# A decoder layer's next low-rank transposition behind the decays' sums, and its gated weights split right behind their scaling

## The chip, the cores and the metric

One core of one Trainium2 chip runs the whole program in one launch. The metric is device microseconds of one execution, all inputs in HBM at its start and all outputs in HBM at its end. The kernel before took 2267.43 us, the median of 3 runs (2267.4 to 2267.67).

## The reference

One layer of a hybrid decoder on 2048 prompt tokens and 8 × 8 sample tokens, model width 1024. One input projection feeds two groups of heads: A is sliding-window attention with rotary positions and a learned sink for each head, B is gated linear attention (GLA: 4 heads, keys of 64, values of 128). Their outputs are joined, projected and added to the input; a squared-ReLU MLP of 4096 follows.

```python
proj = jnp.einsum('btd,de->bte', rms_norm(x, g_mix_pre), w_in)
q, k, v, gq, gk, gv, gr, glr = jnp.split(proj, points, axis=-1)      # glr: 16 columns
attn = swa_banded(q, k, v, sinks)                                    # group A, window 128
log_a = log_sigmoid(einsum('btr,rk->btk', glr, w_gk2) + b_gk) / 16   # GLA's decays, low rank
o, s_new = gla_chunked(gq, gk, gv, log_a, s_init)
gla_out = rms_norm(o, g_gla) * silu(gr)
x = x + rms_norm(concat(attn, gla_out) @ w_out, g_mix_post)
u = relu(rms_norm(x, g_ffn_pre) @ w_up)
x = x + rms_norm((u * u) @ w_down, g_ffn_post)
```

## The kernel before

All is fp32. A product is made of high and low parts: a factor is copied to a rounded type (hi, ACT), the rest is subtracted (lo, DVE or POOL), and three matmuls hi·hi, hi·lo, lo·hi are summed in PSUM. The prompt is 16 tiles of 128 tokens (numbers 0 to 15); the 64 sample tokens are tile 16 (NB).

**The stages.** First the attention stage, to about 342 us: for each tile the input projection of group A (proj), rotary, scores (sc), softmax (s), its transposition (pT), the weighted values (av). Then the GLA stage, to about 790 us. Then output projection, and the MLP's up and down products, the longest part. PE's, ACT's and DVE's order in the attention stage is the order of recording: `te`, `ac` and `dv` chain each instruction to the one before. Instructions issued on `nc.*` directly are placed by the scheduler, by what they depend on and the priority that the place in the program gives. `tc.issue_after(x)` holds a block's priority back behind x.

**The weights of group B in the attention stage.** Their columns are four chunks (c = 0 to 3, limits G_AT; chunk 3, of 400 columns, ends with the 16 low-rank ones). Chunks 3 and 0 (G_EARLY) are prepared during tiles 3 to 10, two pieces of 128 rows in each: `load_gw` asks for a raw piece (two raw buffers, SP's queue), `split_gw` (L264) multiplies it by the norm's gain on POOL (L269) and leaves the copy to hi (ACT) and the subtract to lo (POOL, L273) in the list `gained`; `split_some` (L757), called once in each of a tile's four units, first does what is in `gained`, then takes new pieces, (2, 1, 0, 0) by unit. So the copy and the subtract of a piece follow one call behind its multiply. On POOL there are also the casts of kh and kl (L436 to L447), which bring keys to the other half of the partitions, and the rotary products (L387, L393).

**GLA, one tile.** `decays` makes log-decays for a tile: the 16 low-rank columns of gp are transposed (pg), DVE casts them to glrT (L944), one matmul with w_gk2 gives z, ACT and DVE make the log-sigmoid zt, lh and ll (L953 to L956); `decayed` transposes zt (tT) and copies it to `before` (L1068). `gla(i)` makes keys and queries (gqk), sums decays with a matrix of ones (es) and takes their exp (kd, L1087), starts the output gate (sg, L962 to L971), and then walks seven levels b = 1, 2, … 64: `level_sums` extends the running sums `before` and `after` by adds on DVE (L1012, L1013) and takes exps on ACT (dec), `leveled` multiplies keys and queries by them (XK L994, XQ L998). At L1098 ACT takes the exp of all of `before`, from which DVE makes qd (L1100). The level products are matmuls in four groups (gm_0, gm_2, gm_4, gm_6, two levels each), and each result is put into AT by masked copies on DVE (L1019). Then ds, the state, and o. `following` is the next tile's `decayed`: it is advanced once behind each gm group, so the next tile's pg stands behind gm_0, z behind gm_2, tT behind gm_4.

**What lies between.** Each `yield` hands over to `fill`, which records G_FILL, G_GM matmuls of later tiles' projections to group B (gproj, chunk order 3, 0, 1, 2, tiles 16, 2, 3, … 15), and to `side`, the sample's own GLA (`gla_sample`: its decays are se, its other sums ses). `projecting` evicts a sample chunk in two ACT copies and one DVE add (L619 to L626). The fill ends in tile 13: the first chunk that it projects for tile 14 is not finished when tile 13's sums are recorded.

**Banks.** PSUM has tags a, b, c with two banks each, d and e with one. gproj takes a, the sample b, gm c; gqk, es, pg, z and ds share d; o and ogT share e; tT takes b.

**The output projection** takes its third tile's input by `load_mix`, whose split (hi by ACT, lo by DVE) is recorded while tile 15's levels run.

Of the kernel before, what the change touches and what calls it, by code (L numbers as in the profile page):

```python
# [15 lines left out]
AF = mybir.ActivationFunctionType  # L16
# [5 lines left out]
P = 128  # L22
# [7 lines left out]
HD = 64  # L30
# [95 lines left out]
def f32(ap):  # L126
    return ap.bitcast(F32)
# [23 lines left out]
def hybrid_step_kernel(ctx: ExitStack, tc: tile.TileContext, I, O):  # L151
# [97 lines left out]

    gw, gained = {}, deque()  # L250

# [12 lines left out]
    def split_gw(c, k, raw):  # L264
        hi, lo = (t[:, k, : g_width(c)] for t in gw[c][1:])
        if c in G_LATE:
            split_gained(hi, lo, raw, k)
            return
        nc.gpsimd.tensor_tensor(raw, raw, gcol[:, k : k + 1].to_broadcast([P, g_width(c)]), op=ALU.mult)  # L269

        def rest():
            ac.activation(hi, raw, AF.Copy)
            nc.gpsimd.tensor_tensor(lo, raw, f32(hi), op=ALU.subtract)  # L273

        gained.append(rest)

# [324 lines left out]
    def projecting(i, xT, chunks, act=nc.scalar):  # L601

        n = rows(i)
        for c in chunks:
            p_ = bank([P, 512], "a", f"gproj_{i}_{c}")
            _, wh, wl = gw[c]
# [150 lines left out]
    def split_some(n):  # L757

        while gained:
            gained.popleft()()  # L760
        for _ in range(min(n, len(weights))):
            c, k, raw, stage = weights.popleft()
            split_gw(c, k, raw)
            if stage and late:
                weights.append((*load_gw(*late.popleft(), *stage), stage))
# [171 lines left out]

    def decays(i, gp, n, kind="d"):

        assert {(i, c) for c in range(4)} <= projected or i < NB  # L940
        gt = glrT[i % 2] if i < NB else s_kx[:32, 0, :]
        pg = bank([P, P], kind, f"pg_{i}")
        te.transpose(pg[:16, :n], gp[:n, 1536:1552], ident[:n, :n])
        nc.vector.tensor_copy(gt[:16, :n], pg[:16, :n])  # L944
# [8 lines left out]
        nc.vector.scalar_tensor_tensor(t[:n], z[:n], 0.0, t[:n], op0=ALU.min, op1=ALU.subtract)  # L953
# [61 lines left out]
    def put_level(at, gm, mk, b, n):  # L1015

        dst = halves(at, b)[1]
        m = mk.rearrange("p (m b) -> p m b", b=b).unsqueeze(1).to_broadcast([n, 4, n // (2 * b), b])
        nc.vector.copy_predicated(dst, m, gm.rearrange("p h (m b) -> p h m b", b=b))  # L1019

# [37 lines left out]

    def decayed(i, gp):

        assert (i, 3) in projected
        parts = yield from decays(i, gp, P)
        yield
# [8 lines left out]
    def gla(i, gp, og=iter(())):  # L1072
# [14 lines left out]
        ex = nc.scalar.activation(kd, e_, AF.Exp, scale=1.0 / 16)  # L1087
        nc.gpsimd.tensor_tensor(kd, kd, gp[:, 256:512], op=ALU.mult)
        with tc.issue_after(ex.ins):
            sg = gate(i, gp, P)  # L1090
# [5 lines left out]
        yield G_FILL[1] if i < NB - 1 else G_LAST, 2  # L1096
        following = decayed(i + 1, gps[i + 1]) if i < NB - 1 else iter(())
        nc.scalar.activation(dec[:, :, NL, :], before, AF.Exp, scale=1.0 / 16)  # L1098
# [3 lines left out]
        for l0 in range(0, NL, 2):  # L1102
# [3 lines left out]
            for l in range(l0, min(l0 + 2, NL)):  # L1106
                for g in range(2):
# [5 lines left out]
                    for u, uu in enumerate(half_of):  # L1113
# [3 lines left out]
                        )  # L1117
            next(following, None)
            if l0 == NL - 1:
# [6 lines left out]
            for l in range(l0, min(l0 + 2, NL)):  # L1126
# [5 lines left out]
                for u, uu in enumerate(half_of):  # L1132
                    put_level(at[uu, :, uu], gm[uu, l - l0, :, u * 32 : u * 32 + 32], msk[uu, l, u * 32 : u * 32 + 32], LEVELS[l], HD)
        So, Sn = S[i % 2], S[(i + 1) % 2]
        for g in range(2):
            for r in range(2):
# [3 lines left out]
                    op0=ALU.mult, op1=ALU.add,  # L1140
                )
        yield G_FILL[2], 2
        o_ = bank([P, 4, P], "e", f"o_{i}")
# [17 lines left out]
    def gla_sample(gp):  # L1161
# [9 lines left out]
        qk = qk_T(i, gp, NS, "b")  # L1171
        yield
        for g in range(2):
            e_ = bank([P, (SL + 1) * NS], "b", f"se_{g}")
            te.matmul(e_, lh[:NS, g * P : (g + 1) * P], slev, start=True, stop=False)
            te.matmul(e_, ll[:NS, g * P : (g + 1) * P], slev, start=False, stop=True)
            nc.scalar.activation(s_dec[:, g].rearrange("p l t -> p (l t)"), e_, AF.Exp, scale=1.0 / 16)
        yield
# [60 lines left out]
    def load_mix(i, lo=None, hi=None):  # L1239
        n = rows(i)  # L1240
        if lo is not None:
            nc.sync.dma_start(f32(lo), mix_d[i])
            yield
            split_copy(hi, lo, f32(lo))
            mixes[i] = [[t[:, k, :] for k in range(KT)] for t in (hi, lo)]
# [119 lines left out]

    wo, pre, ogs_of, mixes, raws, late_mix = {}, {}, {}, {}, [], []
    early = []
# [3 lines left out]
    for i in range(NB):  # L1371
        parts = [gla(i, gps[i], ogs_of.pop(i - 1, iter(())))]
        if i == 0:
            parts = [(n or (12, True) for n in decayed(i, gps[i])), *parts]
        for n, free in chain.from_iterable(parts):
# [744 lines left out]
```

## Time and profile before

| | us |
|---|---|
| median of 3 runs | 2267.43 |
| profiled execution | 2268.25 |
| its span | 2266.5 |
| outside the span | 1.75 |
| PE busy | 2203.9 |
| DVE busy | 1621.2 |
| ACT busy | 1202.2 |
| POOL busy | 272.8 |

A row of the timeline has the start, the length of the instruction (or of so many together, x2), the engine, the line, the operation, what it writes and reads, and in brackets the idle time ahead of it and what ended it. L140 is the wrapper of the recorded engines, so there one reads by the tile's name. A row of the waits has total, count and longest. A row of the windows has for each engine its busy time, then the clock that was granted to PE (1.00 is full), the DMA share and GB/s. SPq is SyncE's queue, from which the transfers start.

### The profile page before, as it was taken

The page shows a single profiled execution, that of the slowest core. Times are in us where ns is not written, and L with a number is a line of the kernel's source. Part 1 is how long each engine was busy: PE and PEld are TensorE (multiplying, and loading weights), DVE is VectorE, ACT ScalarE, POOL GpSimd, SP SyncE. Part 2 cuts the span into 40 slices and gives each one's busy share as a digit, 9 for nine tenths or more (in the row PEclk, how much of TensorE's full clock was granted, in tenths as well). Part 3 has the DMA queues.
Part 4 walks back from the last instruction along what each step waited for, and adds up shares of the span by engine and source line. Part 5 has one row for each costly group of instructions (what it writes and reads, how often), then busy time and mean ns, then how long its engine had stood idle before and what let it go on. Part 6 is the DMA issues. An engine that isn't in the chain of part 4 may idle for free.

```text
span 2266.5 us, 34072 instructions
## 1 busy us (share of the span) xinstructions
PE 2203.9 (97%) x11800; PEld 1879.8 (83%) x11800; DVE 1621.2 (72%) x3367; ACT 1202.2 (53%) x2498; POOL 272.8 (12%) x424
## 2 busy tenths in 40 slices
PE   8989999999999999999999999999999999999997
PEld 7888888889998788888888888888888888888886
DVE  5888877888887776687776788878544645755557
ACT  5777764445545444455555565555444444554445
POOL 3466421112112110000000000000000000000000
PEclk9999999999999999999999999999999999999999
DMA  7333332121112355766454666676655755866665
GB/s 235 119 128 133 109 97 64 66 73 52 49 65 71 119 200 177 246 215 234 172 207 173 246 244 227 220 251 228 226 185 179 227 175 185 280 222 219 223 195 196
DMA packets 229938, 392.65 MB, mean 173 GB/s; under 512 B 23057, under 2 KB 137638, under 8 KB 225782
## 3 DMA queue, kind: packets, MB, share of 16 engines
q1 hardware_dynamic: 229766, 390.48, 51.5%
q8 instruction: 93, 1.52, 0.3%
q14 instruction: 79, 0.65, 0.1%
HBM read 255.61 MB, written 135.86 MB: 173 GB/s over the span
## 4 chain that ended last, share of the span: by engine, by line
PE 71%; DVE 16%; ACT 6%; DMA 3%; issue 3%; POOL 1%; SPq 0%; DVEq 0%; ACTq 0%; POOLq 0%
PE dn L140 24%; PE uc L140 7%; PE ua L140 7%; PE gproj L140 7%; PE out L1276 5%; PE ud L140 4%; PE ue L140 3%; PE ub L140 3%; DVE s L140 2%; PE proj L140 2%; DVE AT L1019 1%; PE sam L140 1%; PE dsam L140 1%; PE out L140 1%; DVE pl L140 1%
## 5 line engine op out<-in xcount | busy, mean ns | idle before, releaser
L140 PE MATMUL dn<-ot,os 128*128 128x512 f32 x2688 | 623.8, 390 | 3.6 <-DVE ot L140 2.0
L140 PEld LDWEIGHTS dn<-ot,os 128*128 128x128 f32 x2688 | 503.9, 188 | 113.0 <-DVE ot L140 5.3
L140 DVE TENSOR_TENSOR os<-os 128x512 fp32r<-128x512 f32 x224 | 154.8, 691 | 227.9 <-ACT os L140 227.5
L140 ACT ACTIVATE os<-os 128x512 fp32r<-128x512 f32 x224 | 141.4, 631 | 284.1 <-DMA os<-s_d 233.2
L140 PE MATMUL gproj<-wg,gx 128*128 128x384 f32 (+1 forms) x1408 | 280.7, 349 | 2.1 <-ACT s_dec L621 1.6
L140 PEld LDWEIGHTS gproj<-wg,gx 128*128 128x128 f32 x1408 | 247.8, 191 | 12.9 <-issue 10.7
L140 ACT ACTIVATE st<-st 128x512 f32<-128x512 f32 x225 | 142.3, 633 | 142.0 <-DVE st L140 137.9
L140 PE MATMUL ua<-H,w 128*128 128x512 f32 x744 | 179.8, 390 | 1.0 <-DVE w L140 0.9
L140 PE MATMUL uc<-H,s 128*128 128x512 f32 x744 | 178.8, 389 | 0.0
L140 PEld LDWEIGHTS ua<-H,w 128*128 128x128 f32 x744 | 138.5, 188 | 30.2 <-DVE w L140 1.8
L140 PEld LDWEIGHTS uc<-H,s 128*128 128x128 f32 x744 | 139.5, 188 | 28.9
L216 POOL TENSOR_TENSOR frs<-rs_v,half 128x1 f32<-128x1 f32 (+1 forms) x13 | 8.3, 636 | 1228.9 <-DVE rs_v L140 1228.9
L140 DVE TENSOR_TENSOR st<-st 128x512 f32<-128x512 f32 x160 | 110.4, 692 | 49.2 <-ACT st L140 45.9
L1276 PE MATMUL out<-wo,mt 128*128 128x512 f32 x608 | 141.8, 392 | 0.5 <-DVE mt L227 0.5
L1276 PEld LDWEIGHTS out<-wo,mt 128*128 128x128 f32 x608 | 113.1, 188 | 24.0 <-DVE mt L227 1.0
L140 DVE TENSOR_TENSOR s<-t,s 128x1024 fp32r<-128x1024 f32 x62 | 76.0, 1226 | 34.8 <-ACT s L140 31.7
L140 DVE TENSOR_TENSOR ot<-ot 128x512 fp32r<-128x512 f32 x128 | 88.3, 690 | 15.2 <-ACT ot L140 14.6
L140 ACT ACTIVATE s<-t 128x1024 fp32r<-128x1024 f32 x62 | 65.6, 1059 | 59.8 <-PE ue L140 24.6
L140 PE MATMUL proj<-wa_hi,xh 128*128 128x384 f32 (+1 forms) x272 | 95.5, 354 | 0.9 <-ACT wa_hi L140 0.6
L140 PE MATMUL proj<-wa_lo,xh 128*128 128x384 f32 (+1 forms) x272 | 94.3, 351 | 0.0
L140 PE MATMUL proj<-wa_hi,xl 128*128 128x384 f32 (+1 forms) x272 | 93.0, 346 | 0.0
L140 ACT ACTIVATE ot<-ot 128x512 fp32r<-128x512 f32 x128 | 80.8, 631 | 20.9 <-DMA ot<-t_d 17.1
(407 smaller groups left out, 4112.2 us busy)
## 6 DMA issues: line engine op xcount, KB each, us to landing
os<-s_d SPq DMA_DIRECT2D x224, 256.0 KB, 2.8
s_d<-st SPq DMA_DIRECT2D x31, 1792.0 KB, 8.6
raw<-in_w_up SPq DMA_DIRECT2D x64, 512.0 KB, 6.3
ot<-t_d SPq DMA_DIRECT2D x128, 256.0 KB, 3.5
rt<-in_w_down SPq DMA_DIRECT2D x96, 256.0 KB, 3.1
t<-in_w_down SPq DMA_DIRECT2D x64, 256.0 KB, 3.2
t_d<-t SPq DMA_DIRECT2D x32, 512.0 KB, 7.0
gx<-xt_d SPq DMA_DIRECT2D x28, 512.0 KB, 4.0
```

The lines of the kernel that those rows point to most:

```text
L140: ins = call(*a, **k)
L216: nc.gpsimd.tensor_tensor(out, v[:n], e, op=ALU.pow)
L1019: nc.vector.copy_predicated(dst, m, gm.rearrange("p h (m b) -> p h m b", b=b))
L1276: te.matmul(p_, x, w[:, cc], start=k + u == 0, stop=k == KT - 1 and u == len(products) - 1)
```

## The change

Five edits, no instruction more or less on any engine.

1. A gated weight's copy and subtract are recorded right behind its multiply; the list `gained` is gone.
2. The sample's third projected chunk (c = 1) takes bank e instead of a.
3. If the next tile's chunk 3 is projected (tiles 0 to 12 as i, so pg, z and tT of tiles 1 to 13), its transposition pg is recorded behind es, in a bank of c, and z follows gm_0; gm_2 is passed over; tT stays behind gm_4. For tiles 14 and 15 the order stays pg, z, tT behind gm_0, gm_2, gm_4, with pg in d.
4. The sample's decays se use one bank and one exp of 128 x 512 instead of two banks and two exps.
5. The third tile's split in `load_mix` is issued behind the last masked copy of the tile then at work; `put_level` returns its instruction for that.

```diff
-    gw, gained = {}, deque()
+    gw = {}
...
         nc.gpsimd.tensor_tensor(raw, raw, gcol[:, k : k + 1].to_broadcast([P, g_width(c)]), op=ALU.mult)
-
-        def rest():
-            ac.activation(hi, raw, AF.Copy)
-            nc.gpsimd.tensor_tensor(lo, raw, f32(hi), op=ALU.subtract)
-
-        gained.append(rest)
+        ac.activation(hi, raw, AF.Copy)
+        nc.gpsimd.tensor_tensor(lo, raw, f32(hi), op=ALU.subtract)
...
         for c in chunks:
-            p_ = bank([P, 512], "a", f"gproj_{i}_{c}")
+            p_ = bank([P, 512], "ae"[(i, c) == (NB, G_ORDER[2])], f"gproj_{i}_{c}")
...
     def split_some(n):
 
-        while gained:
-            gained.popleft()()
         for _ in range(min(n, len(weights))):
...
-    def decays(i, gp, n, kind="d"):
+    def decays(i, gp, n, kind="d", ahead=False):
...
-        pg = bank([P, P], kind, f"pg_{i}")
+        pg = bank([P, P], "c" if ahead else kind, f"pg_{i}")
...
-    def decayed(i, gp):
+    def decayed(i, ahead=False):
 
         assert (i, 3) in projected
-        parts = yield from decays(i, gp, P)
+        parts = yield from decays(i, gps[i], P, ahead=ahead)
...
         ex = nc.scalar.activation(kd, e_, AF.Exp, scale=1.0 / 16)
         nc.gpsimd.tensor_tensor(kd, kd, gp[:, 256:512], op=ALU.mult)
+        ahead = (i + 1, 3) in projected
+        following = decayed(i + 1, ahead) if i < NB - 1 else iter(())
+        if ahead:
+            next(following, None)
         with tc.issue_after(ex.ins):
             sg = gate(i, gp, P)
...
         yield G_FILL[1] if i < NB - 1 else G_LAST, 2
-        following = decayed(i + 1, gps[i + 1]) if i < NB - 1 else iter(())
...
-            next(following, None)
+            if not (ahead and l0 == 2):
+                next(following, None)
...
+        e_ = bank([P, 2, (SL + 1) * NS], "b", "se")
         for g in range(2):
-            e_ = bank([P, (SL + 1) * NS], "b", f"se_{g}")
-            te.matmul(e_, lh[:NS, g * P : (g + 1) * P], slev, start=True, stop=False)
-            te.matmul(e_, ll[:NS, g * P : (g + 1) * P], slev, start=False, stop=True)
-            nc.scalar.activation(s_dec[:, g].rearrange("p l t -> p (l t)"), e_, AF.Exp, scale=1.0 / 16)
+            te.matmul(e_[:, g], lh[:NS, g * P : (g + 1) * P], slev, start=True, stop=False)
+            te.matmul(e_[:, g], ll[:NS, g * P : (g + 1) * P], slev, start=False, stop=True)
+        nc.scalar.activation(s_dec.rearrange("p g l t -> p g (l t)"), e_, AF.Exp, scale=1.0 / 16)
...
-            split_copy(hi, lo, f32(lo))
+            with tc.issue_after(puts[0].ins):
+                split_copy(hi, lo, f32(lo))
```

The order on POOL in one tile of the attention stage (around the end of tile 8; wg0_raw2 to 5 are raw pieces, wg0_1 the lo parts), before:

```order
L470 COPY s_8_1_1_2662<-sink_401 128x2
L216 TENSOR_TENSOR rstd_all_175<-rs_v_2659,half_173 128x1
L470 COPY s_9_0_0_2724<-sink_401 128x2
L273 TENSOR_TENSOR wg0_1_188<-wg0_raw2_2577,wg0_0_187 128x384
L273 TENSOR_TENSOR wg0_1_188<-wg0_raw3_2579,wg0_0_187 128x384
L269 TENSOR_TENSOR wg0_raw4_2837<-wg0_raw4_2837,gcol_176 128x384
L269 TENSOR_TENSOR wg0_raw5_2839<-wg0_raw5_2839,gcol_176 128x384
L436 CAST kh_9_2753<-kh_9_2753 64x128 x2
L470 COPY s_9_0_1_2792<-sink_401 128x2
L440 CAST kh_10_3013<-kh_9_2753 128x2x128
L447 CAST kl_9_2754<-kl_9_2754 64x128
```

and now:

```order
L437 CAST kl_9_2754<-kl_8_2494 128x2x128
L466 COPY s_8_1_1_2666<-sink_401 128x2
L271 TENSOR_TENSOR wg0_1_188<-wg0_raw2_2577,wg0_0_187 128x384
L271 TENSOR_TENSOR wg0_1_188<-wg0_raw3_2579,wg0_0_187 128x384
L216 TENSOR_TENSOR rstd_all_175<-rs_v_2663,half_173 128x1
L269 TENSOR_TENSOR wg0_raw4_2837<-wg0_raw4_2837,gcol_176 128x384
L269 TENSOR_TENSOR wg0_raw5_2839<-wg0_raw5_2839,gcol_176 128x384
L466 COPY s_9_0_0_2724<-sink_401 128x2
L432 CAST kh_9_2753<-kh_9_2753 64x128 x2
L466 COPY s_9_0_1_2792<-sink_401 128x2
L436 CAST kh_10_3013<-kh_9_2753 128x2x128
L443 CAST kl_9_2754<-kl_9_2754 64x128
```

The subtracts moved ahead of rstd_all, and with them the point at which the raw buffers come free; the next two multiplies (raw4, raw5) stand ahead of the same casts as before.

PE in GLA tile 10, before (x4, x8: so many alike; `...` are gproj matmuls of the fill; the number behind a name is its tile):

```order
L140 MATMUL es_10_7981<-lh1_4955,c_suf_1525 128x256
L140 MATMUL es_10_7981<-ll1_4957,c_suf_1525 128x256
...
L140 MATMUL gm_10_0_8061<-XQ_4942,qk0_4950 64x2x32 x4
L140 MATMUL gm_10_0_8061<-XQ_4942,XK_4941 64x2x32 x4
L140 MATMUL pg_11_8070<-ident_168,gp_11_7959 16x128
...
L140 MATMUL gm_10_2_8086<-XQ_4942,XK_4941 64x2x32 x8
L140 MATMUL z_11_8095<-wgk_1539,glrT1_4935 128x256
...
L140 MATMUL gm_10_4_8116<-XQ_4942,XK_4941 64x2x32 x8
L140 MATMUL tT_11_8125<-ident_168,zt0_4952 128x128 x2
```

and now:

```order
L140 MATMUL es_10_7979<-lh1_4955,c_suf_1525 128x256
L140 MATMUL es_10_7979<-ll1_4957,c_suf_1525 128x256
L140 MATMUL pg_11_7984<-ident_168,gp_11_7957 16x128
...
L140 MATMUL gm_10_0_8062<-XQ_4942,qk0_4950 64x2x32 x4
L140 MATMUL gm_10_0_8062<-XQ_4942,XK_4941 64x2x32 x4
L140 MATMUL z_11_8071<-wgk_1539,glrT1_4935 128x256
...
L140 MATMUL gm_10_2_8092<-XQ_4942,XK_4941 64x2x32 x8
...
L140 MATMUL gm_10_4_8114<-XQ_4942,XK_4941 64x2x32 x8
L140 MATMUL tT_11_8123<-ident_168,zt0_4952 128x128 x2
```

pg moved ahead of 14 matmuls of the fill, z ahead of 9 of them and of gm_10_2; tT stands where it stood.

DVE in the same tile, before:

```order
L998 TENSOR_TENSOR XQ_4942<-dec0_4947,qk0_4950 64x2x64 x11
L1013 TENSOR_TENSOR before0_4948<-before0_4948 128x2x64
L994 TENSOR_TENSOR XK_4941<-dec0_4947,qk0_4950 128x2x64
L998 TENSOR_TENSOR XQ_4942<-dec0_4947,qk0_4950 64x2x64 x2
L1100 TENSOR_TENSOR qd0_4945<-qk0_4950,dec0_4947 128x256
L966 SCALAR_TENSOR_TENSOR sg0_4943<-gp_10_7682,sg0_4943 128x512
L1019 COPY_PREDICATED AT_4936<-c_0_1527,gm_10_0_8061 64x4x32
L944 COPY glrT1_4935<-pg_11_8070 16x128
L1019 COPY_PREDICATED AT_4936<-c_0_1527,gm_10_0_8061 64x4x32
L1019 COPY_PREDICATED AT_4936<-c_0_1527,gm_10_0_8061 64x4x16x2 x2
L1019 COPY_PREDICATED AT_4936<-c_0_1527,gm_10_2_8086 64x4x8x4 x2
L1019 COPY_PREDICATED AT_4936<-c_0_1527,gm_10_2_8086 64x4x4x8 x2
```

and now:

```order
L1007 TENSOR_TENSOR before0_4948<-before0_4948 128x2x64
...
L992 TENSOR_TENSOR XQ_4942<-dec0_4947,qk0_4950 64x2x64 x2
L1097 TENSOR_TENSOR qd0_4945<-qk0_4950,dec0_4947 128x256
L938 COPY glrT1_4935<-pg_11_7984 16x128
L960 SCALAR_TENSOR_TENSOR sg0_4943<-gp_10_7680,sg0_4943 128x512
L1013 COPY_PREDICATED AT_4936<-c_0_1527,gm_10_0_8062 64x4x32 x2
L1013 COPY_PREDICATED AT_4936<-c_0_1527,gm_10_0_8062 64x4x16x2 x2
L947 SCALAR_TENSOR_TENSOR zt0_4952<-z_11_8071,zt0_4952 128x256
L949 CAST lh0_4954<-zt0_4952 128x256
L950 TENSOR_TENSOR ll0_4956<-zt0_4952,lh0_4954 128x256
```

The last add on `before` (128x2x64) stood behind the XQ rows and is now ahead of the first; the cast to glrT moved ahead of sg and of the first masked copy; zt, lh and ll moved ahead of the masked copies of gm_10_2.

More of the change, by code (lines that the diff above doesn't have):

```diff
@@ L1018, in put_level @@
         m = mk.rearrange("p (m b) -> p m b", b=b).unsqueeze(1).to_broadcast([n, 4, n // (2 * b), b])
-        nc.vector.copy_predicated(dst, m, gm.rearrange("p h (m b) -> p h m b", b=b))
+        return nc.vector.copy_predicated(dst, m, gm.rearrange("p h (m b) -> p h m b", b=b))
     def put_diagonal(i, at, gp, n):
@@ L1132, in gla @@
                 for u, uu in enumerate(half_of):
-                    put_level(at[uu, :, uu], gm[uu, l - l0, :, u * 32 : u * 32 + 32], msk[uu, l, u * 32 : u * 32 + 32], LEVELS[l], HD)
+                    put = put_level(at[uu, :, uu], gm[uu, l - l0, :, u * 32 : u * 32 + 32], msk[uu, l, u * 32 : u * 32 + 32], LEVELS[l], HD)
         So, Sn = S[i % 2], S[(i + 1) % 2]
@@ L1141, in gla @@
                 )
+        puts[0] = put
         yield G_FILL[2], 2
@@ L1364, in products @@
             yield
-    wo, pre, ogs_of, mixes, raws, late_mix = {}, {}, {}, {}, [], []
+    wo, pre, ogs_of, mixes, raws, late_mix, puts = {}, {}, {}, {}, [], [], {}
     early = []
@@ L1373, in hybrid_step_kernel @@
         if i == 0:
-            parts = [(n or (12, True) for n in decayed(i, gps[i])), *parts]
+            parts = [(n or (12, True) for n in decayed(i)), *parts]
         for n, free in chain.from_iterable(parts):
```

## The prediction

> **What bounds the kernel now.** I read the page first, then the sum of TensorE's waits, then the two stages that the change touches in the timeline.
>
> ```profile
> PE 2203.9 (97%) x11800; PEld 1879.8 (83%) x11800; DVE 1621.2 (72%) x3367; ACT 1202.2 (53%) x2498; POOL 272.8 (12%) x424
> ...
> PE 71%; DVE 16%; ACT 6%; DMA 3%; issue 3%; POOL 1%; SPq 0%; DVEq 0%; ACTq 0%; POOLq 0%
> ```
>
> PE is busy for 2203.9 of 2266.5 us: about 63 us of idle time is all that an edit of order can win, plus what the clock loses behind a gap. The change adds no instruction, so each of its terms is a wait of PE.
>
> ```profile
> PE pT L140 <- DVE s L140: 8.3, 17, 1.7
> ...
> PE z L140 <- DVE glrT L944: 4.6, 6, 2.1
> PE sc L140 <- POOL kl L447: 3.4, 5, 0.8
> PE tT L140 <- DVE zt L953: 3.1, 3, 1.4
> PE gm L140 <- DVE AT L1019: 2.8, 2, 2.5
> ```
>
> The columns are total, times, longest. pT and sc belong to the attention stage (to 342 us), which the scaled weights run through; z, tT and gm to the GLA stage (to about 790 us). Nothing is re-ordered after that, so some 1470 us of the span stay as they are.
>
> **The attention stage: weights scaled and copied in one go.** The first scores (sc<-kh,qh) of a tile mark its period:
>
> ```profile
> 102.94 0.36 PE L140 MATMUL sc<-kh,qh 128*128 128x256 f32 x1 [0.26 <-DVE qh L140]
> ...
> 122.68 0.36 PE L140 MATMUL sc<-kh,qh 128*128 128x256 f32 x1 [0.26 <-DVE qh L140]
> ...
> 232.00 0.36 PE L140 MATMUL sc<-kh,qh 128*128 128x256 f32 x1 [0.26 <-DVE qh L140]
> ...
> 249.45 0.36 PE L140 MATMUL sc<-kh,qh 128*128 128x256 f32 x1 [0.17 <-DVE qh L140]
> ...
> 266.92 0.36 PE L140 MATMUL sc<-kh,qh 128*128 128x256 f32 x1 [0.17 <-DVE qh L140]
> ```
>
> Two tiles without weight pieces take (266.92 − 232.00)/2 = 17.46 us. The six tiles with pieces between 122.68 and 232.00 take 109.32, which is 4.56 more than six times 17.46; the one from 102.94 takes 19.74, 2.28 more. One of the six shows why, and 114.95 what went wrong in the slowest tile:
>
> ```profile
> 114.95 0.54 ACT L140 ACTIVATE wg<-wg_raw 128x400 fp32r<-128x400 f32 x1 [1.28 <-POOL wg_raw L269]
> ...
> 116.83 0.38 PE L140 MATMUL av<-ph,vv 128*128 128x256 f32 x1 [1.28 <-ACT ph L140]
> ...
> 184.36 0.60 ACT L140 ACTIVATE ph<-pT 128x512 fp32r<-128x512 f32 x1 [0.92 <-PE pT L140]
> ...
> 188.37 0.94 ACT L140 ACTIVATE wg<-wg_raw 128x384 fp32r<-128x384 f32 x2
> ...
> 188.98 1.98 POOL L273 TENSOR_TENSOR wg<-wg_raw,wg 128x384 fp32r<-128x384 f32 x2
> ...
> 190.02 1.30 SPq L237 DMA_DIRECT2D wg_raw<-in_w_in  x2
> ...
> 192.50 0.83 POOL L269 TENSOR_TENSOR wg_raw<-wg_raw,gcol 128x384 f32<-128x384 f32 x1 [1.54 <-DMA wg_raw<-in_w_in]
> ...
> 194.22 0.83 POOL L269 TENSOR_TENSOR wg_raw<-wg_raw,gcol 128x384 f32<-128x384 f32 x1 [0.89 <-DMA wg_raw<-in_w_in]
> ...
> 196.81 0.38 PE L140 MATMUL sc<-kl,qh 128*128 128x256 f32 x1 [0.77 <-POOL kl L447]
> ```
>
> POOL's subtract frees the two raw buffers at 190, SP then asks for the next two pieces, and POOL stands at the head of its queue in front of the multiplies until they land (1.54 and 0.89 us). The casts of kh and kl are queued behind, and PE waits 0.77 us for kl. In the changed order the copy stands right behind xh's first half, ahead of the ph that began at 184.36, and the request goes to SP ahead of xt_d's stores instead of between them. So copy, subtract and request come some 4 us earlier, the pieces land by about 189 to 190, and the two multiplies (1.66 us) end before the casts. The pair of copies costs ACT 0.94 us where it stood idle for 0.92: covered. Without that cover it would delay ph, and PE behind it, by up to 0.94 us in 8 tiles, 7.5 us. xt_d's stores, now behind the request, lose up to its 1.30 us; their reader is the next stage. I take **−3.6** of the 4.56, since POOL's work still slows some DVE work, with ends of −4.6 and 0. In the slowest tile the multiply ended at about 114.9, and the copies, now a place nearer the tile's start, hold ph up whenever its pieces land late: I leave the 2.28 where it is, with ends of −2.3 and, if the copies' 1.28 us come on top, +1.3. In the later tiles such a wait is far off: from a request at 186 to the next tile's copy (184.4 + 17.5 = 201.9) there are 16 us, of which landing and multiplying took 5 (190.02 to 195.05).
>
> **GLA tile 0 and 1.** Here the transposition pg, the cast to glrT and the gate product z now come early:
>
> ```profile
> 367.70 1.63 DVE L998 TENSOR_TENSOR XQ<-dec,qk 64x128 f32<-64x128 f32 x2
> ...
> 368.80 0.45 PE L140 MATMUL gproj<-wg,gx 128*128 128x400 f32 x1 [1.58 <-ACT s_dec L621]
> ...
> 370.86 0.58 DVE L998 TENSOR_TENSOR XQ<-dec,qk 64x128 f32<-64x128 f32 x2
> ...
> 372.33 0.79 PE L140 MATMUL z<-wgk,glrT 17*128 17x256 f32 x1 [2.09 <-DVE glrT L944]
> ...
> 400.10 0.48 PE L140 MATMUL z<-wgk,glrT 17*128 17x256 f32 x1 [0.57 <-DVE glrT L944]
> ...
> 403.30 0.58 PE L140 MATMUL se<-c,lh 64*128 64x256 f32 x1 [1.16 <-ACT s_qk L982]
> ```
>
> In tile 0 two waits, 1.58 + 2.09 = 3.67 us, lose their cause: the sample's third chunk has bank e to itself, and glrT is cast before the XQ rows. But DVE worked without a pause there, so the tile's masked copies (AT) and zt come hardly earlier, and gm_4 and tT inherit most of the wait in one piece. I count **−1.3** (ends 0 and −3.7). In tile 1 DVE has room, both waits go (the second also because the sample's decays take one bank and one exp): **−1.7** (ends 0 and −1.7). The Trainium skill, SBUF — State Buffer, section Who interferes with whom, says that DVE and GpSimd share one pair of ports and that the holder keeps it for a whole instruction; the trace agrees (the same XQ pair takes 1.63 us beside POOL and 0.58 alone). It speaks against the change where POOL's subtract moves under other DVE work; by it alone the −3.6 above would be about −2.
>
> Behind both gaps the clock falls; the clock is the column after the five busy times (PE, PEld, DVE, ACT, POOL):
>
> ```profile
> 372.00:378.00 6.00, 5.67 (x28) 4.42 (x29) 5.01 (x15) 3.11 (x6) 0.00 (x0) 0.50 0.01 1
> ...
> 402.00:408.00 6.00, 4.84 (x29) 3.88 (x28) 3.78 (x14) 2.18 (x7) 0.79 (x1) 0.56 0.30 93
> 408.00:414.00 6.00, 6.00 (x44) 5.03 (x43) 5.32 (x21) 1.53 (x5) 0.00 (x0) 0.87 0.00 0
> ```
>
> The first fall stays, since tile 0 keeps a gap. The second costs (1 − 0.56 + 1 − 0.87) × 6 = 3.4 us. Its two waits go, but many narrow matmuls of the sample remain there, so I take half, **−1.7** (ends 0 and −3.4).
>
> **GLA tiles 4 and 9 to 12.** Rows of tile 4, of the first PE-bound tile, and of a late one:
>
> ```profile
> 494.14 0.36 PE L140 MATMUL gm<-XQ,XK 128*64 128x64 f32 x5 [0.32 <-DVE AT L1019]
> ...
> 496.25 0.33 PE L140 MATMUL tT<-ident,zt 128*128 128x128 f32 x1 [1.42 <-DVE zt L953]
> ...
> 525.43 0.38 PE L140 MATMUL o<-S,qd 128*128 128x256 f32 x1
> ...
> 537.34 0.43 DVE L1100 TENSOR_TENSOR qd<-qk,dec 128x256 f32<-128x256 f32 x1
> ...
> 538.12 0.28 PE L140 MATMUL pg<-ident,gp 128*16 128x128 f32 x1
> ...
> 595.58 0.38 PE L140 MATMUL o<-S,qd 128*128 128x256 f32 x1
> ...
> 631.38 0.42 ACT L1098 ACTIVATE dec<-before 128x256 f32<-128x256 f32 x1 [4.21 <-DVE before L1013]
> ...
> 635.27 0.31 DVE L944 COPY glrT<-pg 16x128 f32<-16x128 f32 x1
> ...
> 692.43 0.38 PE L140 MATMUL o<-S,qd 128*128 128x256 f32 x1
> ...
> 768.24 0.45 PE L140 MATMUL gm<-XQ,XK 128*64 128x64 f32 x3 [2.46 <-DVE AT L1019]
> ```
>
> Tile 4's tT waited because zt comes from a late z; with z one level pair earlier both waits go: **−1.7** (ends 0 and −1.7). The first o rows of tiles 5, 8 and 12 (525.43, 595.58, 692.43) give periods of 23.38 us while PE is the bound and 24.21 in the last four, 3.3 us lost. There ACT stood 4.21 us in front of an exp whose input, the last add on `before`, DVE did behind eleven XQ rows; kd, sg and, on DVE, the cast at 635.27 queued up behind it, and z behind that. In the new order that add is ahead of all XQ rows, and the cast is ahead of sg. I take **−2.4** of the 3.3 (ends 0 and −3.3).
>
> The price: z now stands right behind the first level pair, where pg stood (538.12). The cast follows qd, so it ends at about 537.34 + 0.43 + 0.31 = 538.08, just in time. I charge **+0.4** for 8 tiles that miss by 0.05 (ends 0 and +4, half a microsecond each). Tiles 14 and 15 keep the old place, and gm's 2.46 us at 768.24 stay: there only a split moves behind it, at nothing, since its reader, the third tile of the output projection, comes 12 us later. If that cover were gone it would cost the split's length, about 1.2 us as an estimate.
>
> **The sum.** −3.6 − 1.3 − 1.7 − 1.7 − 1.7 − 2.4 + 0.4 = −12.0 us. The profiled execution took 2268.25 us, 0.82 above the median of 2267.43; 2268.25 − 12.0 = 2256.25, and 0.82 less is **2255.4** on the scale of the median.
>
> **The rivals.**
> (a) The clock takes back the early tiles. If tile 0's waits join into one gap of about 4 us before tT, PE stands longer at one stretch and the 0.50 window repeats or a second follows. For it: 3.67 us of waits with two starts between them brought 0.50 already. Then tile 0 gives 0 and the second fall stays: −12.0 + 1.3 + 1.7 = −9.0, and one more window at 0.50 costs 3 us: about 2261. The Trainium skill, TensorE: Matmul & The Clock Gate, Part 1: The HAM clock gate, says that an idle window of about 3.4 us halves the clock and that the window runs free of the program. By it the same order can give either; the trace agrees so far as 0.50 goes, but it fell behind 3.67 us in two pieces.
> (b) DVE is the true bound of the GLA stage (16% of the chain against ACT's 6%), so waits come back at gm and tT: only the attention stage and tile 1 gain, −3.6 − 1.7 = −5.3: 2262.
> (c) Slower: z waits in every tile. It is now asked for one level pair (9 large matmuls) earlier, and the cast stands behind qd, which waits for ACT's exp of the decays and so for the last add on `before`. If that chain is late in all 13 tiles, each pays a z wait. The six of today average 4.6/6 = 0.77 us and the longest is 2.09; halfway, 1.43, they come to 13 × 1.43 = 18.6 instead of my 0.4: −12.4 + 18.6 = +6.2, 2273.6. It decides where the cast comes over 12.4/13 = 0.95 us behind z's turn; against it speaks 538.08 beside 538.12.
> (d) More goes: the second fall whole (−3.4), the slowest tile's 2.28 and tile 0's 3.67: −12.0 − 1.7 − 2.3 − 2.4 = −18.4: 2249.
>
> **How the numbers follow.** Forecast 0.52, (a) 0.16, (b) 0.13, (c) 0.05, (d) 0.14. The range runs from (d), 2249, to past (b), 2263.5. A measurement of this kernel can tell about 0.2%, 4.5 us, from no change, so faster means under 2262.9: the forecast, (a), (d) and 0.05 of (b), together 0.87. The same holds the rest of (b) and 0.02 of (c), 0.10; slower is what is left of (c), 0.03.
>
> **What would show it.** Right: tiles of the attention stage at 17.5 to 17.7 us with POOL no longer waiting for wg_raw in front of kh; no z wait over 0.2 us in tiles 2 to 13; o rows 23.4 to 23.6 us apart through tile 12; a gm or tT wait of 2 to 4 us in tile 0. Wrong: ACT waiting for wg_raw in front of ph, z waits in every tile, or an `s` on DVE longer than before under POOL's subtract.

## The result, and the profile after

The changed kernel took 2255.51 us, the median of 6 runs (2253.05 to 2256.07), the kernel before 2266.43 beside it (6 runs, 2264.72 to 2267.67): a ratio of 0.995, with a 95% interval of 0.9937 to 0.9962. The forecast was 2255.4. The profiled execution of the changed kernel took 2253.41 us, 2.1 less than the median, at a mean granted clock of 0.998; the one of before had 0.992. So the two traces are 14.8 us apart, and not 10.9, and what is read from them below is weighed against that.

The page's first line after, and the waits of PE that answer to those shown of before (total, times, longest):

```profile
PE 2193.1 (97%) x11800; PEld 1873.4 (83%) x11800; DVE 1630.6 (72%) x3367; ACT 1202.5 (53%) x2497; POOL 271.4 (12%) x424
```

```profile
PE gm L140 <- DVE AT L1013: 6.2, 2, 3.6
...
PE z L140 <- DVE glrT L938: 3.4, 5, 0.9
...
PE pg L140 <- ACT gp L622: 2.2, 1, 2.2
...
PE tT L140 <- DVE zt L947: 1.3, 1, 1.3
```

sc no longer waits for POOL at all. z still waits five times, but no more than 0.9 us; gm now waits 3.6 us in one piece; and there is a wait that before did not have, pg for an eviction of ACT. The edits take one instruction away: ACT has 2497 where it had 2498, since edit 4 makes one exp of two. DVE's busy time rose by 9.4 us (1621.2 before) with the same 3367 instructions; where that comes from is told with the price of the early z.

The first scores of the same tiles of the attention stage, from the timeline after:

```profile
120.21 0.36 PE L140 MATMUL sc<-kh,qh 128*128 128x256 f32 x1 [0.15 <-DVE qh L140]
...
225.01 0.36 PE L140 MATMUL sc<-kh,qh 128*128 128x256 f32 x1 [0.16 <-DVE qh L140]
...
242.50 0.36 PE L140 MATMUL sc<-kh,qh 128*128 128x256 f32 x1 [0.17 <-DVE qh L140]
...
259.95 0.35 PE L140 MATMUL sc<-kh,qh 128*128 128x256 f32 x1
```

The six tiles with weights now take (225.01 − 120.21)/6 = 17.47 us, as long as the two without (17.47): the whole 4.56 us are gone. One of these tiles shows how:

```profile
178.72 0.93 ACT L140 ACTIVATE wg<-wg_raw 128x384 fp32r<-128x384 f32 x2
...
179.39 1.99 POOL L271 TENSOR_TENSOR wg<-wg_raw,wg 128x384 fp32r<-128x384 f32 x2
...
180.43 1.30 SPq L237 DMA_DIRECT2D wg_raw<-in_w_in  x2
...
183.96 0.83 POOL L269 TENSOR_TENSOR wg_raw<-wg_raw,gcol 128x384 f32<-128x384 f32 x1 [0.27 <-DMA wg_raw<-in_w_in]
...
187.52 0.63 POOL L432 CAST kh<-kh 64x128 fp32r<-64x128 f32 x2 [2.60 <-ACT kh L140]
```

POOL still waits for the pieces (12.3 us in all, 16.0 before), but it is through with them 2.6 us before ACT gives it kh.

The GLA stage after: PE's waits in tiles 0, 5, 7, 8, 9 and 12, and the first o rows of tiles 4 and 8.

```profile
367.56 0.69 PE L140 MATMUL gm<-XQ,XK 128*64 128x64 f32 x16 [3.62 <-DVE AT L1013]
...
486.69 0.59 PE L140 MATMUL o<-S,qd 128*128 128x256 f32 x2
...
496.74 0.63 PE L140 MATMUL ogT<-ident,og 128*128 128x128 f32 x4 [0.74 <-DVE og L1035]
...
501.63 0.66 PE L140 MATMUL z<-wgk,glrT 17*128 17x256 f32 x2 [0.87 <-DVE glrT L938]
...
549.24 0.67 PE L140 MATMUL z<-wgk,glrT 17*128 17x256 f32 x2 [0.58 <-DVE glrT L938]
...
573.85 0.67 PE L140 MATMUL z<-wgk,glrT 17*128 17x256 f32 x2 [0.83 <-DVE glrT L938]
...
584.38 0.59 PE L140 MATMUL o<-S,qd 128*128 128x256 f32 x2
...
598.04 0.66 PE L140 MATMUL z<-wgk,glrT 17*128 17x256 f32 x2 [0.65 <-DVE glrT L938]
...
667.70 0.28 PE L140 MATMUL pg<-ident,gp 128*16 128x128 f32 x1 [2.16 <-ACT gp L622]
```

The first o row of tile 4 before:

```profile
502.11 0.59 PE L140 MATMUL o<-S,qd 128*128 128x256 f32 x2
```

Tile 0 has one gap of 3.62 us where it had 1.58 and 2.09. Tile 4's wait before tT is gone. But the o rows of tiles 4 to 8 are now (584.38 − 486.69)/4 = 24.42 us apart, where it was 23.37 ((595.58 − 502.11)/4), and behind tile 12's sums PE stands for 2.16 us. The clock, in stretches of 6 us around tile 0 (the column behind the five busy times):

```profile
360.00:366.00 6.00, 3.93 (x34) 3.26 (x32) 5.88 (x14) 3.88 (x10) 2.90 (x3) 1.00 0.25 89
366.00:372.00 6.00, 4.45 (x37) 3.95 (x38) 5.29 (x16) 2.39 (x5) 0.00 (x0) 0.75 0.00 0
372.00:378.00 6.00, 6.00 (x41) 5.69 (x40) 5.24 (x13) 2.96 (x11) 2.18 (x2) 0.96 0.01 3
```

The fall behind tile 0 lost (0.25 + 0.04) × 6 = 1.7 us where it had lost 3.4; the one in tile 1 (0.56 and 0.87) did not come at all.

### The profile page after: what moved, and what is told of

It is laid out like the page before. It is cut to its first block, busy times and chain, and to the rows that moved or that the text cites. A ratio compares the mean times of both kernels' runs of the same rounds, so it can differ in the third digit from the quotient of the medians.

```text
span 2251.6 us, 34100 instructions
## 1 busy us (share of the span) xinstructions
PE 2193.1 (97%) x11800; PEld 1873.4 (83%) x11800; DVE 1630.6 (72%) x3367; ACT 1202.5 (53%) x2497; POOL 271.4 (12%) x424
## 4 chain that ended last, share of the span: by engine, by line
PE 70%; DVE 17%; ACT 6%; DMA 3%; issue 3%; POOL 1%; DVEq 0%; SPq 0%; ACTq 0%; POOLq 0%
PE dn L140 24%; PE uc L140 7%; PE ua L140 7%; PE out L1276 6%; PE gproj L140 6%; PE ub L140 4%; PE ue L140 3%; PE ud L140 3%; DVE s L140 2%; PE proj L140 2%; PE sam L140 1%; DMA os<-s_d 1%; DVE XQ L992 1%; PE dsam L140 1%; PE out L140 1%
## 5 line engine op out<-in xcount | busy, mean ns | idle before, releaser
L140 PEld LDWEIGHTS gproj<-wg,gx 128*128 128x128 f32 x1408 | 243.9, 188 | 12.1 <-issue 9.8
L140 DVE TENSOR_TENSOR ot<-ot 128x512 fp32r<-128x512 f32 x128 | 88.2, 689 | 15.6 <-ACT ot L140 14.8
L140 ACT ACTIVATE s<-t 128x1024 fp32r<-128x1024 f32 x62 | 65.6, 1059 | 59.8 <-PE ue L140 24.6
```

The lines of the kernel that those rows point to most:

```text
L140: ins = call(*a, **k)
```

## The experiments

Times are medians; the ratio stands against runs of the kernel before on the same chip. The mean clock is the mean over a kernel's runs of the granted clock. It varies from run to run, and the time with it: the 71 runs of the kernel before in the three comparisons below took 2267.9 us on average where the clock was 0.992 (15 runs), 2266.2 at 0.993 (34), 2264.9 at 0.994 (17) and 2261.1 at 0.995 (4), with one more at 0.991, about 1.8 us for each 0.001. The last two columns split a difference, taken against the runs of before in the same comparison, by that slope. They are an estimate, and name no cause: a wait can itself lower the clock. For the change the clock of most runs of before beside it is not known, and 0.9931 is assumed.

| kernel | us | ratio, 95% | mean clock | by the clock | the rest |
|---|---|---|---|---|---|
| before | 2266.05 | 1 | 0.9931 | | |
| the change | 2255.51 | 0.995 (0.9937 to 0.9962) | 0.9965 | −6.1 | −4.8 |
| edit 1 alone | 2259.12 | 0.9972 (0.9963 to 0.9981) | 0.9941 | −1.8 | −5.1 |
| edit 3 alone | 2266.06 | 1.0002 (0.9993 to 1.0012) | 0.9942 | −2.0 | +2.0 |
| edits 2, 4 alone | 2266.94 | 1.0009 (1.0001 to 1.0018) | 0.9932 | −0.2 | +1.1 |
| all but edit 1 | 2265.34 | 0.9998 (0.9988 to 1.0008) | 0.9946 | −2.7 | +1.6 |
| all but edit 3 | 2261.55 | 0.998 (0.9971 to 0.9989) | 0.9935 | −0.7 | −3.5 |
| all but edit 5 | 2257.82 | 0.9963 (0.9951 to 0.9976) | 0.9956 | −4.5 | −3.4 |
| z behind gm_2 | 2259.42 | 0.9972 (0.9963 to 0.9981) | 0.9949 | −3.2 | −3.4 |
| tile 13 in the old place | 2255.18 | 0.9959 (0.9944 to 0.9974) | 0.9960 | −5.2 | −6.1 |
| sums first | 2254.10 | 0.9952 (0.9939 to 0.9965) | 0.9960 | −5.2 | −7.2 |
| sums first, z behind gm_2 | 2254.55 | 0.9946 (0.9933 to 0.9958) | 0.9946 | −2.7 | −8.5 |
| extra matmuls in tile 0 | 2259.53 | 0.9975 (0.9965 to 0.9984) | 0.9955 | −4.3 | −2.7 |
| pg in bank d | 2272.75 | 1.0032 (1.002 to 1.0043) | 0.9922 | +1.6 | +5.4 |

### Parts of the change

**Edit 1 alone.** The diff is edit 1 as shown with the change, on the kernel before.

> Only edit 1: copy and subtract of a gated weight right behind its multiply; the rest as before. If the attention stage is all of it, the trace after puts the gain there at 4.5 us in the six tiles with weights and 0.5 each in the first two, so about -5.5 us and tiles of 17.46; the term of the prediction (-3.6, tiles of 17.6) would give about -3.6. Rival: the shorter attention stage only shifts the GLA stage against the clock's windows, and the time moves by another 2 us in either direction with the same tiles of 17.46.

It gave −6.9 us, with the six tiles at 17.45 to 17.48 us and the slowest at 19.13, as in the trace of the whole change. So the attention stage is worth 5 to 6 us by itself, and more than the prediction's term.

**Edit 3 alone.** The diff is edit 3 on the kernel before.

> Only edit 3: the next tile's transposition behind the sums, the gate product at gm_0. If the GLA gain is this edit's, -4 to -6 us, with z waits of 0.6 to 0.9 us in tiles 5 to 9 and a pg wait of about 2 us for tile 13 as in the trace after; the 1.58 us wait of the fill for the sample's second copy in tile 0 stays. Rival: the early tiles' gain comes from the sample's edits, then -1 to -2 us only.

Nothing was gained, where 4 to 6 us were expected. Its timeline in tile 1:

```profile
400.74 0.38 PE L140 MATMUL se<-c,lh 64*128 64x256 f32 x1 [0.58 <-DVE lh L955]
...
402.21 0.38 PE L140 MATMUL se<-c,ll 64*128 64x256 f32 x1 [1.09 <-DVE ll L956]
...
403.65 0.58 PE L140 MATMUL se<-c,lh 64*128 64x256 f32 x1 [1.05 <-ACT s_qk L982]
```

With the prompt's chain ahead, the sample's sums wait 2.7 us where they waited 1.16, of which 0.16 are left in the trace after, with edit 4, and at most 1.10 in the other traces that have both. The z and pg waits are the ones of the whole change.

**Edits 2 and 4 alone.** The diff is these two edits on the kernel before.

> Only edits 2 and 4: the sample's third chunk in bank e, its decays in one bank with one exp. By the prediction the 1.58 us in tile 0 move on to z and gm, and part of the 1.16 us before se goes: -0.5 to -1.5 us. Rival (the clock): with these waits gone the clock's falls behind tiles 0 and 1 go too, -4 us or more.

Nothing again, or 1 us lost. The wait of 1.58 us in tile 0 is gone, and z there waits 3.94 us, which is the old 1.58 and 2.09 and 0.3 more: the prediction's picture of one gap, without the early cast.

**All but edit 1, all but edit 3, all but edit 5.** Each is the changed kernel with that edit undone; without edit 3 it reads

```diff
-        ahead = (i + 1, 3) in projected
+        ahead = False
```

> The changed kernel without edit 1 (edits 2 to 5 alone). Edit 1 alone took 6.9 us off the median and the whole change 10.9, while edit 3 alone and edits 2 and 4 alone took nothing. If the GLA edits work only together (the sample's waits behind se, 2.7 us with edit 3 alone, need edit 4, and tile 0's early cast needs edit 2), this gives -3 to -5 us against before. Rival: edit 5 or the clock's windows make the rest, and it gives 0 to -1.

> The changed kernel without edit 3 (edits 1, 2, 4 and 5). Edit 1 alone gave 2259.1 at a mean clock of 0.994, edits 2 and 4 alone nothing, all five 2255.5 at 0.9965. If edit 3's gain is only that the clock falls less often behind tiles 0 to 2, this is at 2258 to 2260 with a clock of 0.994 and no z wait at all in tiles 5 to 9. Rival: edit 3 is worth nothing even so, and it is at 2255 to 2256.

> The changed kernel without edit 5: the third tile's split is placed where the scheduler puts it. The prediction has it at nothing: the same within 1 us, with gm's wait of 2.5 us in tile 15 as before. Rival: edit 5 is what took the clock's fall behind that wait away (0.50 at 768 before, none after), and without it 1 to 2 us are lost.

Edits 2 to 5 without edit 1 gained nothing that can be told (2265.34), so the expectation of −3 to −5 us was wrong and the rival nearer. Its trace has the GLA waits of the change (gm 3.63, z 0.8 at most, pg 2.17) and the attention stage of before, with the slowest tile at 20.81 us, in which the clock fell (0.64 and 0.79 in two stretches of 3 us). On top of edit 1 the same four edits are worth 3.6 us (2259.12 and 2255.51); why they need edit 1 for that is not shown. Without edit 3 it took 2261.55: on top of the other edits, edit 3 is worth about 6 us, and most of it goes with the clock (0.9935 to 0.9965). Without edit 5 it took 2257.82, 2.3 us more. The intervals overlap, but its five runs lie at 2256.03 and above and the six of the change at 2256.07 and below, in different comparisons. Its trace shows the same wait of 2.59 us in tile 15 and no fall of the clock behind it, so the rival's mechanism is not seen; whether edit 5 is worth its 1 to 2 us stays open.

### The wait for z

**z behind gm_2**, pg early as in the change:

```diff
-            if not (ahead and l0 == 2):
+            if not (ahead and l0 == 0):
                 next(following, None)
```

> The changed kernel with the gate product z back behind gm_2, the transposition pg still early. Theory (a loop): with z at gm_0 and tT left at gm_4, the way from a tile's tT through DVE's sums, qd and the cast to the next z and tT is longer than PE's own 23.4 us, so PE waits 0.6 to 0.9 us at z in tiles 5 to 9; at gm_2 these waits are gone and the o rows of tiles 5 to 8 are 23.4 us apart, -2 to -3 us there, and tT waits of 1.4 us may return at tile 4 or 5. Rival (DVE is simply full): the waits come back at gm or tT with the same size and the periods stay at 24.1 to 24.6. In tiles 9 to 12 the last add on `before` is late again in this order, which costs up to 2.4 us by the prediction's term. Together 2253 to 2257.

The o rows of tiles 4 and 8, its waits for z and tT, and the rows of tiles 11 and 12:

```profile
493.87 0.59 PE L140 MATMUL o<-S,qd 128*128 128x256 f32 x2
...
587.86 0.38 PE L140 MATMUL o<-S,qd 128*128 128x256 f32 x1
...
659.32 0.59 PE L140 MATMUL o<-S,qd 128*128 128x256 f32 x2
...
687.05 0.59 PE L140 MATMUL o<-S,qd 128*128 128x256 f32 x2
```

```profile
PE tT L140 <- DVE zt L947: 5.1, 6, 1.5
PE pg L140 <- ACT gp L622: 2.5, 1, 2.5
...
PE z L140 <- DVE glrT L938: 0.8, 2, 0.4
```

Tiles 5 to 8 are (587.86 − 493.87)/4 = 23.50 us apart: DVE is not simply full, and with z behind gm_2 the waits for z are gone there. But tT's waits came back (5.1 us, six times), and tile 12 took 27.73; of that 1.7 are a fall of the clock at 673 us. The whole took 3.9 us more than the change and missed the 2253 to 2257 that were expected; by the estimate 2.9 of the 3.9 go with the clock.

**Tile 13 in the old place, and the sums first.** The first takes the early pg away from tile 13; the second leaves it and records all adds ahead of the products, so that the last add comes early:

```diff
-        ahead = (i + 1, 3) in projected
+        ahead = i < 12 and (i + 1, 3) in projected
```

```diff
             level_sums(before, after, dec, l, b)
+        for l, b in enumerate(LEVELS):
             leveled(XK if l else None, XQ, dec, qk, l, b, P)
```

> The changed kernel, but tile 13's transposition keeps the old place behind gm_0 (ahead only while i < 12). In the trace after, that pg waits 2.16 us for ACT's eviction of the chunk which it reads, queued behind the exp that waits for the last add on `before`, and that tile takes 25.86 us instead of 24.52. Theory: placed right behind es it is asked for before its input is there, so with the old place the wait goes and the kernel gains 1 to 2 us against the change. Rival: z of tile 13 waits instead (0.5 us in the trace before), and nothing is gained.

> The changed kernel with all adds on `before` and `after` and their exps recorded ahead of all XK and XQ products, so that the last add comes early in tiles 12 and 14 too (in tile 15 not). If ACT's head-of-queue wait for that add is what makes pg wait 2.16 us in tile 12 and tT 1.3 us later, both go: -2 to -3 us against the change. Rival: the first level pair's products come later by the adds moved ahead of them, gm_0 waits in the DVE-bound tiles 0, 1 and 15, and it comes out slower by 1 to 3 us.

Where the 2.16 us come from is seen in ACT's rows of the changed kernel just ahead of that pg:

```profile
666.74 0.42 ACT L1095 ACTIVATE dec<-before 128x256 f32<-128x256 f32 x1 [5.58 <-DVE before L1007]
667.07 0.57 ACT L622 ACTIVATE gp<-gproj,rstd_all 128x400 f32<-128x400 f32 x1
```

pg reads the chunk that the second row evicts, and that row stood behind an exp which waited 5.58 us for the last add. With the sums first the wait is gone and tile 12 took 23.53 us instead of 25.86; with the old place it took 24.18, and z waited 0.52 there. In the totals (2254.10 and 2255.18 beside 2255.51) neither can be told from the change, and the 2 to 3 and 1 to 2 us that were expected did not show.

**Both: sums first, z behind gm_2.**

> All adds recorded ahead of the products, as in e8_sums_first, and z back behind gm_2, as in e4_z_at_gm2; pg still early. If the two costs of the change in the GLA stage are z asked for at gm_0 (0.6 to 0.9 us in tiles 5 to 9) and the late last add (tile 13's pg), both are gone here and the o rows are 23.4 to 23.6 us apart from tile 4 on: 2250 to 2252.5, the fastest of all. Rival: z behind gm_2 brings tT's waits back (1.2 to 1.5 us in tiles 2 and 5 of e4_z_at_gm2) and the sums ahead make gm_0 wait in tiles 0 to 3, and it stays at 2254 or above.

Its o rows of tiles 5, 9, 10 and 13:

```profile
517.04 0.59 PE L140 MATMUL o<-S,qd 128*128 128x256 f32 x2
...
611.01 0.59 PE L140 MATMUL o<-S,qd 128*128 128x256 f32 x2
...
634.52 0.59 PE L140 MATMUL o<-S,qd 128*128 128x256 f32 x2
...
704.99 0.59 PE L140 MATMUL o<-S,qd 128*128 128x256 f32 x2
```

(611.01 − 517.04)/4 = 23.49 and (704.99 − 634.52)/3 = 23.49: all late tiles run at PE's pace, and by the estimate it has the lowest rest of all (−8.5). But its mean clock is lower (0.9946), and the median of 2254.55, above the 2250 to 2252.5 expected, cannot be told from that of the change. One run, at a clock of 0.997, took 2249.6.

### The gap in tile 0, and the bank

**Extra matmuls.** 16 matmuls of 384 columns, result unused, stand ahead of tile 0's gm_4:

```diff
+            if i == 0 and l0 == 4:
+                warm, w0 = bank([P, 512], "e", "warm"), gw[0][1]
+                for n in range(16):
+                    te.matmul(warm[:, :384], w0[:, n % KT, :P], w0[:, n % KT, :384], start=True, stop=True)
             gm = bank([P, 2, 4, P // 2], "c", f"gm_{i}_{l0}")
```

> The changed kernel with 16 extra matmuls (128x384, result unused) right ahead of gm_4 in tile 0, where PE stands idle for 3.6 us. If the granted clock falls because of that gap (0.75 and 0.96 in two stretches of 6 us, 1.7 us lost), the fall is gone and tiles 0 and 1 gain 1 to 2 us; more in runs in which the fall took two windows. Rival: DVE is the bound there anyway, PE's slower stretch is hidden, and the extra 3 us of matmuls change nothing or cost up to 0.5 us. The order on DVE shifts by some twenty rows in tile 1, which may move it by about 1 us either way.

The last two of the three stretches shown above, and PE's waits in tile 0 and behind it:

```profile
366.00:372.00 6.00, 5.14 (x50) 4.34 (x49) 5.69 (x16) 2.72 (x6) 0.00 (x0) 1.00 0.01 3
372.00:378.00 6.00, 3.81 (x23) 3.30 (x24) 5.53 (x15) 2.45 (x7) 2.64 (x2) 1.00 0.00 0
```

```profile
368.45 0.69 PE L140 MATMUL gm<-XQ,XK 128*64 128x64 f32 x16 [0.86 <-DVE AT L1013]
...
375.31 1.16 PE L140 MATMUL o<-gp,AT 128*128 128x128 f32 x8 [0.87 <-ACT AT L1132]
...
377.79 0.66 PE L140 MATMUL gqk<-ident,gp 128*128 128x128 f32 x4 [1.32 <-DVE S L1140]
```

The clock stayed at 1.00, gm_4 still began 12.1 us behind es as in the change (368.45 − 356.33, 367.56 − 355.46), and PE waited twice more, for ACT's share of AT and for DVE's S. The rival's mechanism held: the fall behind tile 0 was hidden behind DVE. Its price did not: the rival had at most 0.5 us, and the median lost 4 us against the change, 2.2 of them in the trace in tile 1 (29.40 us from o to o instead of 27.17). The order of some twenty DVE rows in tile 1 moved with it, so the reason for the loss is not settled.

**pg in bank d.**

```diff
-        pg = bank([P, P], "c" if ahead else kind, f"pg_{i}")
+        pg = bank([P, P], kind, f"pg_{i}")
```

> The changed kernel with the early transposition pg in bank d, as before, instead of a bank of the level products. Theory: d then holds es, and pg has to wait until ACT has taken kd from it; in the trace of before pg behind gm_0 waited 0.3 us for that in tiles 10 and 12, and 14 fill matmuls (2.6 us) earlier it should wait 0.5 to 2 us in nearly every tile, z behind it too: 5 to 15 us slower than the change. Rival: ACT takes kd at once, and it is the same within 1 us.

```profile
PE pg L140 <- ACT kd L1081: 15.2, 13, 4.1
```

pg waits in all 13 tiles, for the exp that empties es's bank: 0.73 us in most, 4.09 in tile 1. 15.2 us of waits, 17 us of time more than the change, 0.3% slower than before. In this kernel the early transposition in es's bank costs more than the early place wins.

## Why the prediction was right, and where it was wrong

The median was forecast to 0.1 us, but not by its terms, and the forecast was −12.0 us from a median of 2267.43, where −10.9 were measured beside 2266.43. Point by point, from the traces of before and after:

- **Attention stage (−3.6).** The mechanism was right, the size too small: −4.5 in the six tiles, since POOL's work slowed nothing that PE waits for. The slowest tile, which the prediction left at 19.74, took 19.15, and the first 17.45 instead of 17.97: about −5.6 in all, confirmed by edit 1 alone. ACT waited for the late multiply there as forecast (1.46 us at 108.73, 1.28 before). The rule of the Trainium skill, SBUF — State Buffer, section Who interferes with whom, by which alone the term was −2, did not decide here: no tile with weight pieces became longer, and DVE was busy for 92.2 us in the six tiles where it had been for 92.9.
- **Tile 0 (−1.3).** Right: one gap, 3.62 us at gm_4, and from es to o 19.47 us instead of 20.99, −1.5. That gm_4 waits for DVE at either clock is shown by the extra matmuls.
- **Tile 1 and the second fall of the clock (−1.7 − 1.7).** From o to o 27.17 instead of 31.36, −4.2: both waits and, in that run, the whole fall. That part is a draw: of seven other traces with edits 2 to 4 (pg in bank d left out), two have no fall in tiles 1 and 2, one has a fall in tile 1, and five have one in tile 2, between 416 and 433 us.
- **Tile 4 (−1.7).** Both waits went, 25.96 instead of 27.75, but the time came back one tile later: tile 5 took 25.57 instead of 23.32. DVE was still behind, and PE waited 0.74 us for og and 0.87 for z (rows at 496.74 and 501.63).
- **The price of the early z (+0.4).** This step failed. Tiles 5 to 8 took 584.38 − 486.69 = 97.7 us instead of 93.5, +4.2, the far end of its range; 2.25 of it is tile 5. It went wrong in "just in time": the margin of 0.04 us was read where z was asked for one level pair later, and it did not hold once the places had moved. In tile 7 after:

```profile
548.47 0.43 DVE L1097 TENSOR_TENSOR qd<-qk,dec 128x256 f32<-128x256 f32 x1
548.82 0.27 DVE L938 COPY glrT<-pg 16x128 f32<-16x128 f32 x1
...
551.87 1.29 POOL L964 TENSOR_TENSOR sg<-sg,ggla 128x512 f32<-128x512 f32 x1
...
552.02 1.29 DVE L949 CAST lh<-zt 128x256 fp32r<-128x256 f32 x1
...
554.62 0.44 PE L140 MATMUL tT<-ident,zt 128*128 128x128 f32 x2
...
556.09 0.41 DVE L1062 COPY before<-tT 128x256 f32<-128x256 f32 x1
```

  and the same cast before, in tile 6:

```profile
543.04 0.29 DVE L955 CAST lh<-zt 128x256 fp32r<-128x256 f32 x1
```

  The cast to glrT ended at 549.09, and z's turn was at 548.66, where gm_0 ended. Follow the round from one tile's z through tT, its copy, DVE's sums and qd to the cast and the next z. z moved ahead, but tT did not: from z to the copy of tT there are now 18 fill matmuls and two level groups, 5.85 us at the least where it was 3.5 (540.53 to 544.03). With DVE's 17.1 to 17.4 us from that copy to qd's end, 0.19 for the cast and 0.14 until z, the order alone makes a round of 23.3 to 23.6 us, and PE has 23.4 to 23.5 to do: no slack is left. The rounds that begin in tiles 6, 7 and 8 took 24.2, 24.6 and 24.2 us, and what goes beyond is a DVE row that now ran beside POOL's gate product. In tile 7 the cast lh took 1.29 us instead of 0.29 and ended 0.15 us behind POOL's row; tT was there at 555.06, and DVE came to its copy 1.0 us later. In tile 8 it was the same cast (0.9 us late), in tile 6 the row pr (1.40 us instead of 0.45, 0.5 late). Where the copy followed tT within 0.13 us, in tiles 5, 9 and 10, the rounds are 23.5 and 23.6 us long. Over tiles 5 to 12 lh and pr took 6.3 us more than before, two thirds of the rise in DVE's busy time. With z behind gm_2 the waits for z went, but there the cast does not meet POOL's row either (0.29 us in each of these tiles), so that run does not separate the order from the collision; that the collision makes most of the excess is read from the trace, not tried. The prediction reckoned with DVE and POOL in each other's way in the attention stage only.
- **Tiles 9 to 12 (−2.4).** Tiles 9 to 11 won 1.0 us, tile 12 lost 1.3, so the term failed too. The prediction said that the last add is ahead of all XQ rows; in tile 12 it is not, and pg, asked for 2.6 us earlier, stood 2.16 us behind the eviction of its own chunk, a wait that was not on the list.
- **Edits 4 and 5, tiles 14 and 15.** In tile 15 gm waited 2.59 us where it was 2.46, as forecast; that edit 3 without edit 4 lengthens the waits before se was not forecast.

Tile 3 (27.29 us instead of 28.62) and tile 13 (23.42 instead of 24.43) won 2.3 us that no term had. Even so tiles 3 to 13 together took 271.5 us where they had taken 271.1: there the change moved waits about and won nothing. The two failed steps cost some 6.5 us against the forecast. What made up for them in these two traces is, besides tiles 3 and 13, the attention stage with 2 us more than its term, and stretches that no term was about: 1.5 us in the attention stage's first tile and 1.3 in tile 15, where the trace of before has a fall of the clock and the one after has none, and 1.7 behind tile 15. That the sum came out so close is luck.

Over the runs the mean clock rose from 0.9931 to 0.9965, which by the slope is worth about 6 us; the prediction counted 1.7. Where in the stage it comes from is only partly shown: of the six falls in the trace of before (at 41, 372, 403, 430, 464 and 768 us) the trace after has one, at 369; both have one more at the program's very end. Other traces with edits 1 to 4 (pg in bank d left out) have some more, at 39 to 40, 112, 398, 417 to 422, 454 to 456, 673 and 756 to 764 us. The fall near 40 us lies ahead of the first weight piece that edit 1 moves; ten of the fourteen traces have it, among them that of "sums first", which differs from the change only in the GLA stage. So a part of the difference between the two traces is chance. How far the other falls follow from the edits and how far from the place of the program in the clock's windows stays open. The Trainium skill, TensorE: Matmul & The Clock Gate, Part 1: The HAM clock gate, says that the window runs free of the program; that the runs of one kernel beside each other differ by 0.001 to 0.004 in clock and by 3 to 10 us in time agrees with it.

## What to carry to other kernels

Before a wait is counted as gone because a step of a chain was moved ahead, add up the round from one tile to the next (engine by engine, with the place of each step in the queue) and compare it with the bound's period. Then look at what each moved row will run beside: here the order used up the slack, and one cast beside a POOL row made the wait. Compare the tiles behind the one that gained, too: tile 4's 1.8 us came back in tile 5. An early request needs its own buffer, and its input has to be followed back through the queue of the engine that writes it. And where waits let a clock fall, look at the mean clock of many runs next to the time: here more than half of the gain came with it by estimate, and an edit that gained nothing alone was worth 6 us beside the others, most of it by that estimate with the clock.

## What the hardware showed

A wait of 4.09 us (pg in bank d, tile 1) was followed by some 20 us at half clock, although PE was busy all that time; stretches of 4 us:

```profile
384.00:388.00 4.00, 0.05 (x1) 0.00 (x0) 3.87 (x18) 2.79 (x10) 0.31 (x1) 0.95 0.00 0
388.00:392.00 4.00, 3.86 (x11) 2.67 (x12) 2.67 (x7) 2.21 (x6) 0.73 (x1) 0.50 0.17 66
...
404.00:408.00 4.00, 4.00 (x27) 3.19 (x26) 1.66 (x8) 0.60 (x1) 0.00 (x0) 0.50 0.32 120
408.00:412.00 4.00, 4.00 (x30) 3.29 (x29) 3.53 (x12) 1.51 (x5) 0.00 (x0) 0.99 0.00 0
```

The Trainium skill, TensorE: Matmul & The Clock Gate, Part 1: The HAM clock gate, says that the full clock comes back after at least one busy window of about 3.4 us; here it took about six of them, so one was not enough. Behind the gaps of 3.6 to 3.9 us in tile 0 the clock was back after one or two. Why this one took longer was not tried.

The cast lh of 128x256 took 0.27 to 0.30 us each time in the trace of before. In the trace after it began while POOL's second gate product ran (128x512, 1.27 to 1.36 us) in eight tiles, and in each of them it ended 0.15 us behind POOL's row, so that it took up to 1.32 us.
